# A split-weight decoder trunk on one core: weight low parts, bias steps and rotary products move to VectorE, and the planner gives VectorE and GpSimd one SBUF port

## The chip, the core and the metric

The kernel runs on one core of a Trainium2 chip. TensorE (PE) multiplies, VectorE (DVE), ScalarE (ACT) and GpSimd (POOL) do the elementwise work, and SyncE (SP) issues the loads. The metric is the device time of one execution in microseconds; lower is better.

## The reference

Two layers work on 256 tokens of width 1024. Each layer is a token mixer between two half-step SwiGLU blocks of inner width 2816.

```python
def swiglu(h, wg, wu, wd):
    return (jax.nn.silu(h @ wg) * (h @ wu)) @ wd

for i in range(DEPTH):                       # DEPTH = 2
    x = x + 0.5 * swiglu(rmsnorm(x, ffn_norm1[i]), ffn1_wg[i], ffn1_wu[i], ffn1_wd[i])
    h = rmsnorm(x, mix_norm[i])
    x = x + (sliding_window_attention(h, ...) if i % 2 == 0 else latent_attention(h, ...))
    x = x + 0.5 * swiglu(rmsnorm(x, ffn_norm2[i]), ffn2_wg[i], ffn2_wu[i], ffn2_wd[i])
```

Mixer A (layer 0) is causal attention over a window of 128 with 16 query heads and 2 key heads of 64, per-head norms of queries and keys, a sink per head, and a bias per head that depends on the distance of two positions through 32 buckets. Mixer B (layer 1) is latent attention: queries and keys/values come from low-rank projections (256 and 128 wide), each head has 64 plain and 32 rotary columns, and the rotary part is turned by the position:

```python
    q = rmsnorm(q, q_gain)
    q = jnp.concatenate([q[..., :QK_NOPE], apply_rope(q[..., QK_NOPE:], pos)], axis=-1)
```

## The kernel before

**Numbers.** Matrix products keep float32 accuracy by splitting. `weight` (L352) loads a weight tile of 128x1024 into `raw`; ScalarE rounds it into the high part `whi` (L371), and the remainder is the low part `wlo = raw - whi` (L366). Three matmuls (high by high, high by low, low by high) stand for one product. There are 301 such tiles: six per chunk of 256 inner columns in 44 chunks (264), and 37 in the mixers. `raw` has 5 buffers, `whi` and `wlo` 8 each.

**Stages.** In the trace they follow each other: first SwiGLU from 0 to about 250 us, mixer A from about 250 to 313, second SwiGLU to about 500, third SwiGLU to about 690, mixer B to about 785, last SwiGLU to the end. A SwiGLU starts with a norm for each tile of 128 tokens (L653 squares, L661 sum, L664 reciprocal root as a power on GpSimd, L672 scaled copy `p`, L640 transposes, L614/L686 high and low part `xs`), then runs chunk 0 for each tile apart (`th` L779, `h` L781) and chunks 1 to 10 for both tiles together (matmuls L807 and L753).

**Order.** `Plan` takes all operations with their engine, cost, operands and buffers, and schedules them ahead of time: at each step the ready operation with the earliest start plus penalty goes next on its engine. Every engine then runs its own list in that order, so an operation that waits holds up all that stands behind it on its engine. An operation with two engines goes to the one where it ends first. For low parts these are

```python
LOENG = ("DVE", "POOL")
op(LOENG, (c_dve(m), c_pool(m)), low, [(raw, key_), (hi, key_)], [(lo, key_)], seq="wlo", pen=pen, prio=pr, name="W")
```

and the plan sent 254 of the 301 to VectorE and 47 to GpSimd. The plan knows the engines as independent.

**Bias.** Mixer A's bias is made during the first SwiGLU. `keys` (L526) turns positions into thresholds `dk` and differences `df` on GpSimd. `split_bias` (L511) splits the difference table `relb` into three bf16 parts on GpSimd and copies them into the block diagonal of `bdiag` (L518). `bias_ops` then makes 0/1 steps: for query tile 0 with 32 compares of 128x128 (L559), for tile 1 with 32 pairs L562 and L564, all on VectorE. In each of 8 groups 24 small matmuls (L575) multiply steps by `bdiag`; L582 adds the mask.

**Rotary part.** `rope_tables` (L429) makes cosine and sine products with the gains on GpSimd. In `mixer_b` the query projection is copied out of PSUM with all 384 columns (L608 or L612) into `t`, and `rope` does four products and sums on GpSimd (L1179 twice, L1182, L1184) for each of 8 groups of four heads. The key's rotary part is scaled on GpSimd (L1146).

Of the kernel before, what the change touches and what calls it, by code (L numbers as in the profile page):

```python
# [277 lines left out]
def kernel(  # L278
# [110 lines left out]
    def rope_tables():  # L389
# [42 lines left out]
        for t in range(NT):  # L432
            for nm, g in (("q", gq), ("k", gk)):
                cc, ss = const([P, ROPE], f"cc{nm}{t}"), const([P, ROPE], f"ss{nm}{t}")

                def tables(t=t, g=g, cc=cc, ss=ss):
                    g1, g2 = g[:, HD : HD + HALF], g[:, HD + HALF : DQK]
                    sn, cs = scs[:, t, 0, :], scs[:, t, 1, :]
                    G.tensor_tensor(out=cc[:, :HALF], in0=g1, in1=cs, op=ALU.mult)
                    G.tensor_tensor(out=cc[:, HALF:], in0=g2, in1=cs, op=ALU.mult)  # L440
                    G.tensor_tensor(out=ss[:, HALF:], in0=g1, in1=sn, op=ALU.mult)
                    G.tensor_tensor(out=ss[:, :HALF], in0=g2, in1=sn, op=ALU.mult)
                    G.tensor_scalar(
# [53 lines left out]
    def bias_consts():  # L497
# [26 lines left out]
        qidx = buf("clo0", [P, P])  # L524
        dma(0.5, lambda: pi.t, positions[0].partition_broadcast(P), [pi], 1.0)

        def keys():
            G.tensor_copy(out=posq.t, in_=pi.t)
            pv = posq.rearrange("p (t k j) -> p t k j", t=NT, j=4)
            for j in range(4):  # L530
                sl = slice(j * NBKT, (j + 1) * NBKT)
# [4 lines left out]
                G.tensor_tensor(out=df[sl], in0=pv[sl, 0, :, j], in1=pv[sl, 1, :, j], op=ALU.subtract)  # L536
            G.iota(qidx.t, pattern=[[1, P]], base=0, channel_multiplier=0, allow_small_or_imprecise_dtypes=True)

        op("POOL", 3.5, keys, [pi, cols], [posq, dk, df, qidx], pen=1.0)
        K.update(bd=bd, posq=posq, dk=dk, df=df, qidx=qidx)  # L540
# [3 lines left out]
    def bias_ops(t, grp):  # L544


        q, dk, df, qidx, cols, bd = (K[n] for n in ("posq", "dk", "df", "qidx", "cols", "bd"))
# [1 line left out]
        n = 4 if t == 0 else 2
        for i0 in range(0, 8, n):  # L550
            ms = [buf("bm", [P, P]) for _ in range(n)] if t else []

            def fn(i0=i0, ms=ms):
                for i in range(i0, i0 + n):
# [795 lines left out]
```

## Time and profile before

| what | before |
|---|---|
| median of three runs | 980.85 us (979.95 to 980.9) |
| profiled execution | 979.95 us, of which the span of instructions is 978.2 us |
| TensorE busy | 935.4 us, 96% of the span |
| VectorE busy | 624.7 us, 64% |
| ScalarE busy | 474.8 us, 49% |
| GpSimd busy | 197.1 us, 20% |
| memory read | 157.92 MB, 163 GB/s over the span |

Busy time is what an engine spends in instructions; an engine that is busy throughout sets the end, and the idle time of the others costs nothing by itself. The granted clock is the share of TensorE's full speed that it was given in a stretch.

### The profile page before, as it was taken

The page shows a single profiled execution, that of the slowest core. Times are in us where ns is not written, and L with a number is a line of the kernel's source. Part 1 is how long each engine was busy: PE and PEld are TensorE (multiplying, and loading weights), DVE is VectorE, ACT ScalarE, POOL GpSimd, SP SyncE. Part 2 cuts the span into 40 slices and gives each one's busy share as a digit, 9 for nine tenths or more (in the row PEclk, how much of TensorE's full clock was granted, in tenths as well). Part 3 has the DMA queues.
Part 4 walks back from the last instruction along what each step waited for, and adds up shares of the span by engine and source line. Part 5 has one row for each costly group of instructions (what it writes and reads, how often), then busy time and mean ns, then how long its engine had stood idle before and what let it go on. Part 6 is the DMA issues. An engine that isn't in the chain of part 4 may idle for free.

```text
span 978.2 us, 16592 instructions
## 1 busy us (share of the span) xinstructions
PE 935.4 (96%) x6318; PEld 841.0 (86%) x6318; DVE 624.7 (64%) x1161; ACT 474.8 (49%) x814; POOL 197.1 (20%) x218
## 2 busy tenths in 40 slices
PE   5979999999799999999999999999998989999998
PEld 3869989998666899999979999999887869999997
DVE  6588985566866765656576565646689575455552
ACT  5534353545665444444355443545688445354440
POOL 4275430105302110000020000000596021011010
PEclk8999999999889999999999999999999989999999
DMA  7655556564402585656554666564413175656541
GB/s 258 202 160 155 173 174 214 161 197 139 151 1 69 171 259 160 208 170 209 179 173 149 197 196 192 173 212 147 156 53 92 60 234 166 213 163 204 165 150 44
DMA packets 119630, 160.04 MB, mean 164 GB/s; under 512 B 9264, under 2 KB 102912, under 8 KB 119552
## 3 DMA queue, kind: packets, MB, share of 16 engines
q1 hardware_dynamic: 119552, 159.00, 51.7%
q8 instruction: 49, 0.80, 0.3%
q14 instruction: 29, 0.24, 0.1%
HBM read 157.92 MB, written 1.05 MB: 163 GB/s over the span
## 4 chain that ended last, share of the span: by engine, by line
PE 84%; DVE 6%; POOL 4%; issue 3%; ACT 2%; DMA 0%; SPq 0%; POOLq 0%; DVEq 0%; ACTq 0%
PE w L807 44%; PE acc L753 23%; PE w L640 2%; PE acc L707 2%; PE acc L708 2%; PE acc L709 2%; PE w L709 2%; PE w L707 2%; PE w L708 2%; DVE p L672 1%; PE w L1014 1%; DVE p L559 1%; POOL wlo L366 1%; POOL st L599 1%; DVE wlo L366 1%
## 5 line engine op out<-in xcount | busy, mean ns | idle before, releaser
L807 PE MATMUL w<-xs,whi 128*128 128x256 f32 x2560 | 456.3, 281 | 0.0
L807 PEld LDWEIGHTS w<-xs,whi 128*128 128x128 f32 x2560 | 393.1, 188 | 2.8
L366 DVE TENSOR_TENSOR wlo<-raw,whi 128x1024 fp32r<-128x1024 f32 (+3 forms) x254 | 309.9, 1236 | 99.8 <-ACT whi L371 99.2
L371 ACT CAST whi<-raw 128x1024 fp32r<-128x1024 f32 (+3 forms) x301 | 310.1, 1039 | 124.2 <-PE acc L753 91.4
L807 PE MATMUL w<-xs,wlo 128*128 128x256 f32 x1280 | 357.0, 279 | 0.0
L807 PEld LDWEIGHTS w<-xs,wlo 128*128 128x128 f32 x1280 | 241.5, 189 | 0.0
L366 POOL TENSOR_TENSOR wlo<-raw,whi 128x1024 fp32r<-128x1024 f32 (+1 forms) x47 | 120.6, 2575 | 253.6 <-ACT whi L371 231.3
L813 ACT ACTIVATE th<-w 128x256 f32<-128x256 f32 x80 | 30.7, 383 | 201.5 <-PE w L807 201.4
L815 DVE SCALAR_TENSOR_TENSOR th<-th,w 128x256 f32<-128x256 f32 x80 | 33.4, 418 | 133.1 <-ACT th L813 133.1
L753 PE MATMUL acc<-whi,pT 128*128 128x512 f32 x352 | 113.2, 395 | 0.0
L753 PE MATMUL acc<-wlo,pT 128*128 128x512 f32 x352 | 112.7, 394 | 0.0
L753 PE MATMUL acc<-whi,t 128*128 128x512 f32 x352 | 112.3, 392 | 0.0
L753 PEld LDWEIGHTS acc<-wlo,pT 128*128 128x128 f32 x352 | 66.4, 189 | 15.2
L753 PEld LDWEIGHTS acc<-whi,t 128*128 128x128 f32 x352 | 66.0, 188 | 15.6 <-DVE t L626 0.4
L753 PEld LDWEIGHTS acc<-whi,pT 128*128 128x128 f32 x352 | 63.3, 188 | 11.5
L608 ACT CAST pT<-h 128x256 fp32r<-128x256 f32 x80 | 32.5, 406 | 64.5 <-DVE h L817 64.1
L821 DVE TENSOR_TENSOR t<-h,pT 128x256 fp32r<-128x256 f32 x80 | 39.3, 491 | 36.4 <-ACT pT L608 36.4
L664 POOL TENSOR_TENSOR rstd<-var,mhalf 128x1 f32<-128x1 f32 x8 | 4.4, 550 | 233.3 <-DVE var L661 233.3
L699 POOL TENSOR_TENSOR var<-ss 128x1 f32<-128x1 f32 x4 | 0.8, 195 | 205.1 <-ACT junk L653 205.1
L640 PE MATMUL w<-ident,p 128*128 128x128 f32 x160 | 27.4, 309 | 14.4 <-DVE p L672 12.3
L640 PEld LDWEIGHTS w<-ident,p 128*128 128x128 f32 x160 | 20.4, 156 | 22.8 <-DVE p L672 14.8
L707 PE MATMUL w<-whi,xs 128*128 128x512 f32 (+2 forms) x96 | 39.3, 409 | 0.6 <-DVE xs L614 0.6
(186 smaller groups left out, 952.6 us busy)
## 6 DMA issues: line engine op xcount, KB each, us to landing
raw<-in_ffn_wd_dram SPq DMA_DIRECT2D x88, 512.0 KB, 4.4
raw<-in_ffn_wg_dram SPq DMA_DIRECT2D x175, 256.0 KB, 3.9
raw<-in_ffn_wu_dram SPq DMA_DIRECT2D x175, 256.0 KB, 4.2
raw<-in_a_w_in_dram SPq DMA_DIRECT2D x10, 512.0 KB, 4.5
raw<-in_a_w_out_dram SPq DMA_DIRECT2D x8, 512.0 KB, 3.6
raw<-in_b_w_out_dram SPq DMA_DIRECT2D x8, 512.0 KB, 3.6
raw<-in_b_w_in_dram SPq DMA_DIRECT2D x4, 416.0 KB, 3.6
raw<-in_b_w_uq_dram SPq DMA_DIRECT2D x4, 384.0 KB, 3.6
```

The source lines that it names most:

```text
L366: (V if e == "DVE" else G).tensor_tensor(out=lo[:, c], in0=raw[:, c], in1=hi.t.bitcast(F32)[:, c], op=ALU.subtract)
L371: op("ACT", c_act(m), lambda c=c: A.copy(out=hi[:, c], in_=raw[:, c]), [(raw, key_)], [(hi, key_)], seq="wh", pen=pen, prio=pr, name="W")
L608: A.copy(out=o(), in_=i())
L640: T.transpose(out=dst[:rows, i * P : (i + 1) * P], in_=src(i), identity=ident.t)
L707: T.matmul(o, lhsT=hi, rhs=wh, start=start, stop=False)
L708: T.matmul(o, lhsT=hi, rhs=wl, start=False, stop=False)
L709: T.matmul(o, lhsT=lo, rhs=wh, start=False, stop=stop)
L753: T.matmul(acc[nh].t, lhsT=a[:, ft, t0 : t0 + P], rhs=wt[:, nh * 512 : (nh + 1) * 512], start=(c == 0 and ft == 0 and i == 0), stop=(final ...
L807: T.matmul(o, lhsT=wt[:, sl], rhs=xs[:, p, :, kt], start=(kt == j == i == 0), stop=(kt == KT - 1 and j == 1 and i == 2))
L813: op("ACT", c_act(FC, 0.05), lambda th=th, ps=ps: A.activation(th.t, ps[:, :FC], AF.Tanh, scale=0.5), [ps], [th], name=nm)
L815: op("DVE", 0.345, lambda th=th, ps=ps: V.scalar_tensor_tensor(out=th.t, in0=th.t, scalar=1.0, in1=ps[:, :FC], op0=ALU.add, op1=ALU.mult), ...
L821: op("DVE", 0.36, lambda h=h, hthi=hthi, htlo=htlo, fb=fb: V.tensor_tensor(out=htlo[:, fb], in0=h.t, in1=hthi[:, fb].bitcast(F32), op=ALU. ...
```

## The change

The low part has one engine now, VectorE. The plan gets one more resource: an operation of GpSimd, or one of VectorE that reads nothing from PSUM, doesn't start before the last such operation of the other engine has ended. The rotary tables, `keys`, `split_bias`, the query's rotary part and the key's rotary scaling go from GpSimd to VectorE. The query's rotary products read PSUM, so the copy takes 256 columns in place of 384. The steps of tile 0 are one compare of 128x1024 for each of 4 groups. Those of tile 1 are, for each of 8 half groups, four `Sign` and four `Identity` activations of 128x128 on ScalarE (64 in all) and one compare of 128x512 on VectorE. Lines of the changed kernel stand 7 to 16 further down: L366 is L373 there, L559 is L567, L575 is L591, L614 is L630, L672 is L688.

```diff
-LOENG = ("DVE", "POOL")
+BSPEN = 2.0
...
+        o.port = not any((b[0] if isinstance(b, tuple) else b).tag in ("w", "acc0", "acc1") for b in r)
...
+            if e == "POOL" or (e == "DVE" and o.port):
+                s = max(s, self.port["DVE" if e == "POOL" else "POOL"])
             done = s + cost + (POOLPEN if e == "POOL" and len(alts) > 1 else 0.0)
...
-                op(LOENG, (c_dve(m), c_pool(m)), low, [(raw, key_), (hi, key_)], [(lo, key_)], seq="wlo", pen=pen,
+                op("DVE", c_dve(m), low, [(raw, key_), (hi, key_)], [(lo, key_)], seq="wlo", pen=pen,
...
         def split_bias():
+            V.tensor_scalar(out=blk.t, in0=qidx[:, :4], scalar1=cols[:, 1:2], scalar2=None, op0=ALU.is_equal)
             for i, b16 in enumerate(parts):
-                G.tensor_copy(out=b16.t, in_=r.t)
+                V.tensor_copy(out=b16.t, in_=r.t)
                 if i < 2:
-                    G.tensor_tensor(out=r.t, in0=r.t, in1=b16.t, op=ALU.subtract)
-                for j in range(4):
-                    sl = slice(j * NBKT, (j + 1) * NBKT)
-                    G.tensor_copy(out=bd[sl, i, :, j], in_=b16[sl, :])
-
-        op("POOL", 3.5, split_bias, [], [r, bd] + parts, pen=1.0, name="bd")
+                    V.tensor_tensor(out=r.t, in0=r.t, in1=b16.t, op=ALU.subtract)
+                V.tensor_tensor(out=bd[:, i], in0=b16.t.unsqueeze(2).broadcast_to([P, H, 4]),
+                                in1=blk.t.unsqueeze(1).broadcast_to([P, H, 4]), op=ALU.mult)
+
+        op("DVE", 1.0, split_bias, [cols, qidx], [r, bd, blk] + parts, pen=1.0, name="bd")
...
+        if t == 0:
+            op("DVE", c_dve(1024), lambda: V.tensor_tensor(
+                out=steps.t, in0=qt(8), in1=heads(dk[:, 0, grp * 8 : grp * 8 + 8], 8, P), op=ALU.is_ge),
+               [q, dk], [steps], pen=BSPEN, name="bs")
+        for i0 in (0, 4) if t else ():
+            m = buf("p", [P, 4, P])
+
+            def fn(i0=i0, m=m):
+                for i in range(4):
+                    k = grp * 8 + i0 + i
+                    A.activation(m[:, i], qidx.t, AF.Sign, bias=nj[:, k : k + 1])
+                for i in range(4):
+                    k = grp * 8 + i0 + i
+                    A.activation(m[:, i], m[:, i], AF.Identity, bias=df[:, k : k + 1], scale=hd[:, k : k + 1])
+
+            op("ACT", 8 * c_act(P, 0.02), fn, [nj, qidx, df, hd], [m, (steps, i0)], pen=BSPEN, name="bs")
+            op("DVE", c_dve(512), lambda i0=i0, m=m: V.tensor_tensor(
+                out=steps[:, i0 : i0 + 4], in0=qt(4), in1=m.t, op=ALU.is_ge),
+               [q, m], [(steps, i0)], pen=BSPEN, name="bs")
...
-            op("POOL", 0.36, lambda: G.tensor_tensor(
+            op("DVE", 0.2, lambda: V.tensor_tensor(
                 out=kn[:, :, HD:], in0=heads(rr[:, :4], 4, ROPE),
...
-            op(AV, (0.37, 0.47), copy_scaled(lambda: qn.t, qv), [qb], [qn], name=name)
+            op(AV, (0.26, 0.34), copy_scaled(lambda: qn[:, :, :HD], lambda: qv()[:, :, :HD]), [qb], [(qn, 0)], name=name)
...
-                    G.tensor_tensor(
-                        out=tmp[:, :, a0 : a0 + HALF], in0=qn[:, :, HD + b0 : HD + b0 + HALF],
+                    V.tensor_tensor(
+                        out=tmp[:, :, a0 : a0 + HALF], in0=qv()[:, :, HD + b0 : HD + b0 + HALF],
```

What the plan makes of it on VectorE just ahead of the first bias matmuls, before: the compares L559 stand in front of the copy of the table (`relb`, L508) and the rest of `split_bias` is on GpSimd.

```order
L559 TENSOR_SCALAR p<-chi_562,dk 128x128 x24
L815 SCALAR_TENSOR_TENSOR th<-th,w 128x256
L817 TENSOR_TENSOR h<-w,th 128x256
L559 TENSOR_SCALAR p<-chi_562,dk 128x128 x4
L821 TENSOR_TENSOR t_700<-h,pT 128x256
L559 TENSOR_SCALAR p<-chi_562,dk 128x128 x4
L508 COPY relb<-w 128x16
L366 TENSOR_TENSOR wlo<-raw,whi 128x1024 x2
```

In the change the same table is copied and split on VectorE before the first `th` of chunk 1:

```order
L517 COPY relb<-w 128x16
L373 TENSOR_TENSOR wlo<-raw,whi 128x1024
L524 TENSOR_SCALAR blk<-clo_106,cols 128x4
L526 CAST relb_473<-relb 128x16
L528 TENSOR_TENSOR relb<-relb,relb_473 128x16
L529 TENSOR_TENSOR bdiag<-relb_473,blk 128x64
...
L526 CAST relb_475<-relb 128x16
L529 TENSOR_TENSOR bdiag<-relb_475,blk 128x64
L373 TENSOR_TENSOR wlo<-raw,whi 128x1024 x2
L831 SCALAR_TENSOR_TENSOR th<-th,w 128x256
```

So `bdiag` is complete two chunks earlier in VectorE's list, and no longer behind the compares. The first bias group itself stands 48 L807 matmuls later in TensorE's list than before.

On GpSimd around the two norms of the first SwiGLU, before: a low part stands right behind the reciprocal root of tile 0, and four more behind that of tile 1.

```order
L664 TENSOR_TENSOR rstd_137<-var_132,mhalf 128x1
L366 TENSOR_TENSOR wlo<-raw,whi 128x1024
L664 TENSOR_TENSOR rstd_217<-var_213,mhalf 128x1
L366 TENSOR_TENSOR wlo<-raw,whi 128x1024 x4
L528 CAST chi_562<-chi_504 128x256
```

In the change the two roots follow each other, and nothing of 128x1024 is left in GpSimd's list; the other three SwiGLU blocks read alike.

```order
L680 TENSOR_TENSOR rstd_140<-var_135,mhalf 128x1
L680 TENSOR_TENSOR rstd_220<-var_216,mhalf 128x1
L485 TENSOR_SCALAR nsink<-sink 128x16
L487 TENSOR_SCALAR ka<-gcol 128x1
L499 MEMSET kb 128x1
```

On VectorE where mixer B ends and the last SwiGLU begins (L626 makes `xs` low parts, L924 and, in the change, L940 add the mixer's output into `x`), before:

```order
L892 TENSOR_SCALAR p<-p,st 128x256 x2
L626 TENSOR_TENSOR xs<-acc_8254,xs 128x512
L612 CAST xs<-acc_8445 128x512
L626 TENSOR_TENSOR xs<-acc_8445,xs 128x512
L366 TENSOR_TENSOR wlo<-raw,whi 128x1024
L626 TENSOR_TENSOR xs<-acc_8508,xs 128x512
L924 TENSOR_TENSOR x_64<-acc_8386,x_64 128x512
```

The low part shown is one of the eight of `b_w_out`; of the others VectorE's list held two 15 and 7 rows ahead of it and two more than a hundred rows ahead, and GpSimd's list three. In the change all eight stand here in VectorE's list:

```order
L373 TENSOR_TENSOR wlo<-raw,whi 128x1024
L900 RECIPROCAL st<-st 128x4
L908 TENSOR_SCALAR p<-p,st 128x256 x2
L373 TENSOR_TENSOR wlo<-raw,whi 128x1024 x4
L642 TENSOR_TENSOR xs<-acc_8396,xs 128x512
L373 TENSOR_TENSOR wlo<-raw,whi 128x1024 x3
L940 TENSOR_TENSOR x_64<-acc_8431,x_64 128x512
```

They moved from two engines and a spread of places to one engine and one place, beside the 72 matmuls that use them.

## Rows read from the trace of the kernel before

**Rows 1.** The page's chain that ended last, shares of the span by engine

```profile
PE 84%; DVE 6%; POOL 4%; issue 3%; ACT 2%; DMA 0%; SPq 0%; POOLq 0%; DVEq 0%; ACTq 0%
```

**Rows 2.** Windows by stage: length, busy us (instructions) of each engine, granted clock, DMA share, GB/s

```profile
0.00:30.00 30.00, 18.43 (x58) 13.45 (x59) 18.03 (x38) 16.22 (x29) 13.44 (x20) 0.89 0.70 228
30.00:75.00 45.00, 38.41 (x280) 35.29 (x279) 32.34 (x71) 18.26 (x26) 22.46 (x35) 0.94 0.63 194
75.00:222.00 147.00, 147.00 (x1158) 136.32 (x1158) 109.08 (x202) 65.09 (x91) 40.81 (x39) 1.00 0.56 178
...
255.00:285.00 30.00, 24.42 (x105) 16.53 (x104) 24.45 (x112) 16.70 (x66) 5.23 (x3) 0.77 0.16 51
...
313.00:330.00 17.00, 13.98 (x59) 10.72 (x58) 15.97 (x24) 7.98 (x12) 7.79 (x4) 0.90 0.60 185
...
705.00:735.00 30.00, 27.12 (x186) 23.66 (x186) 26.09 (x85) 25.50 (x71) 28.01 (x52) 1.00 0.24 72
735.00:760.00 25.00, 22.41 (x202) 18.89 (x202) 23.74 (x77) 21.31 (x60) 15.26 (x17) 1.00 0.35 106
...
785.00:808.00 23.00, 18.67 (x90) 15.40 (x89) 17.21 (x24) 9.58 (x17) 5.12 (x2) 0.85 0.70 218
```

**Rows 3.** Waits of TensorE: line, what it waited for, us in total, times, longest

```profile
PE w L640 <- DVE p L672: 12.3, 7, 3.5
PE w L575 <- POOL bdiag L518: 6.6, 3, 3.3
PE w L1014 <- DVE st L857: 4.7, 1, 4.7
...
PE w L640 <- DVE h L781: 3.9, 2, 3.4
```

**Rows 4.** Timeline of VectorE: start, us, operation [idle before <-releaser]

```profile
15.75 5.04 DVE L672 TENSOR_SCALAR p<-x,rstd 128x512 f32<-128x512 f32 x2 [0.67 <-POOL rstd L664]
...
256.70 1.25 DVE L857 SCALAR_TENSOR_TENSOR st<-st,nsink 128x4 f32<-128x4 f32 x1
257.98 2.27 DVE L860 TENSOR_TENSOR st<-sink,st 128x4 f32<-128x4 f32 x1
260.17 0.15 DVE L857 SCALAR_TENSOR_TENSOR st<-st,nsink 128x4 f32<-128x4 f32 x1
...
771.54 0.88 DVE L672 TENSOR_SCALAR p<-x,rstd 128x512 f32<-128x512 f32 x2 [0.66 <-POOL rstd L664]
```

**Rows 5.** Timeline of GpSimd at the same two places

```profile
15.69 4.83 POOL L366 TENSOR_TENSOR wlo<-raw,whi 128x1024 fp32r<-128x1024 f32 x2
...
255.57 4.65 POOL L366 TENSOR_TENSOR wlo<-raw,whi 128x1024 fp32r<-128x1024 f32 x2
```

**Rows 6.** Groups of VectorE by form: busy us, mean ns | idle before

```profile
L366 DVE TENSOR_TENSOR wlo<-raw,whi 128x1024 fp32r<-128x1024 f32 x245 | 301.5, 1248 | 98.5 <-ACT whi L371 97.9 <-PE w L807 0.2
...
L562 DVE TENSOR_SCALAR bm<-clo,cols,df 128x128 f32<-128x128 f32 x32 | 16.0, 500 | 0.0
L564 DVE SCALAR_TENSOR_TENSOR p<-bm,dk,chi 128x128 bf16<-128x128 f32 x32 | 15.5, 485 | 1.1
...
L559 DVE TENSOR_SCALAR p<-chi,dk 128x128 bf16<-128x128 f32 x32 | 11.0, 418 | 1.7 <-POOL dk L532 1.7
...
L582 DVE TENSOR_TENSOR S<-w,upper 128x128 f32<-128x128 f32 x16 | 3.5, 279 | 0.0
...
L1143 DVE TENSOR_TENSOR knb<-acc,st 128x256 f32<-128x256 f32 x8 | 3.4, 421 | 1.1 <-POOL st L599 0.9
...
L612 DVE COPY S<-w 96x512 f32<-96x512 f32 x3 | 2.0, 681 | 0.5 <-PE w L640 0.5
```

**Rows 7.** Groups of GpSimd by form, the same columns

```profile
L366 POOL TENSOR_TENSOR wlo<-raw,whi 128x1024 fp32r<-128x1024 f32 x46 | 118.8, 2591 | 253.6 <-ACT whi L371 231.3 <-PE w L807 16.6 <-PE w L709 5.2
L599 POOL TENSOR_TENSOR st<-st,mhalf 128x4 f32<-128x4 f32 x16 | 16.8, 1062 | 2.4 <-DVE st L884 0.9 <-DVE st L1140 0.8 <-DVE st L1172 0.7
```

**Rows 8.** One group of ScalarE by form, the same columns

```profile
L610 ACT ACTIVATE xs<-w,gcols 128x128 fp32r<-128x128 f32 x52 | 14.9, 366 | 21.6 <-PE w L640 16.9 <-DVE xs L614 4.7
```

More of the change, by code (lines that the diff above doesn't have):

```diff
@@ L91 @@
     __slots__ = ("eng", "cost", "fn", "deps", "bufs", "prio", "seq", "end", "tail", "pen", "name", "users", "nd",
-                 "eng_used")
+                 "eng_used", "port")
     def __init__(self, **k):
@@ L220, in run @@
         self.ticks = {}
+        self.port = {"DVE": 0.0, "POOL": 0.0}
         while left:
@@ L261, in run @@
             o.end = free[e] = s + cost
+            if e == "POOL" or (e == "DVE" and o.port):
+                self.port[e] = o.end
             for b in o.bufs:
@@ L438, in tables @@
                     sn, cs = scs[:, t, 0, :], scs[:, t, 1, :]
[L439 to L443, printed above, removed]
+                    V.tensor_tensor(out=cc[:, :HALF], in0=g1, in1=cs, op=ALU.mult)
+                    V.tensor_tensor(out=cc[:, HALF:], in0=g2, in1=cs, op=ALU.mult)
+                    V.tensor_tensor(out=ss[:, HALF:], in0=g1, in1=sn, op=ALU.mult)
+                    V.tensor_tensor(out=ss[:, :HALF], in0=g2, in1=sn, op=ALU.mult)
+                    V.tensor_scalar(
                         out=ss[:, :HALF], in0=ss[:, :HALF], scalar1=-1.0, scalar2=None, op0=ALU.mult
                     )
-                op("POOL", 0.8, tables, [g, scs], [cc, ss], pen=1.0)
+                op("DVE", 0.45, tables, [g, scs], [cc, ss], pen=1.0)
                 K[f"cc{nm}", t], K[f"ss{nm}", t] = cc, ss
@@ L531, in keys @@
                 sl = slice(j * NBKT, (j + 1) * NBKT)
-                G.tensor_scalar(
+                V.tensor_scalar(
                     out=dk[sl], in0=pv[sl, :, :, j], scalar1=cols[sl, 0:1], scalar2=None, op0=ALU.add
                 )
[L536 to L540, printed above, removed]
+                V.tensor_tensor(out=df[sl], in0=pv[sl, 1, :, j], in1=pv[sl, 0, :, j], op=ALU.subtract)
+            V.tensor_scalar(out=nj.t, in0=cols[:, 1 : 1 + P // 4], scalar1=-1.0, scalar2=0.5, op0=ALU.mult, op1=ALU.add)
+            V.tensor_scalar(out=hd.t, in0=df.t, scalar1=0.5, scalar2=None, op0=ALU.mult)
+            V.tensor_tensor(out=df.t, in0=dk[:, 1], in1=hd.t, op=ALU.subtract)
+        op("DVE", 1.6, keys, [pi, cols], [posq, dk, df, nj, hd], pen=1.0)
+        K.update(bd=bd, posq=posq, dk=dk, df=df, qidx=qidx, nj=nj, hd=hd)
         K["bias0"] = buf("S8", [P, H, P])
@@ L544, in bias_ops @@
     def bias_ops(t, grp):
-        q, dk, df, qidx, cols, bd = (K[n] for n in ("posq", "dk", "df", "qidx", "cols", "bd"))
+        q, dk, df, qidx, nj, hd, bd = (K[n] for n in ("posq", "dk", "df", "qidx", "nj", "hd", "bd"))
         steps = buf("p", [P, 8, P], BF16)
[L549 to L554, printed above, removed]
-                    kk = grp * 8 + i
-                    d = dk[:, t, kk : kk + 1]
-                    qt = q[:, t * P : (t + 1) * P]
-                    if t == 0:
-                        V.tensor_scalar(out=steps[:, i], in0=qt, scalar1=d, scalar2=None, op0=ALU.is_ge)
-                    else:
-                        m = ms[i - i0].t
-                        V.tensor_scalar(out=m, in0=qidx.t, scalar1=cols[:, 1 + kk : 2 + kk],
-                                        scalar2=df[:, kk : kk + 1], op0=ALU.is_lt, op1=ALU.mult)
-                        V.scalar_tensor_tensor(
-                            out=steps[:, i], in0=m, scalar=d, in1=qt, op0=ALU.add, op1=ALU.is_le
-                        )
-            op("DVE", n * (0.15 if t == 0 else 0.645), fn, [q, dk, df, qidx, cols], [(steps, i0)] + ms, pen=0.5, name="bs")
@@ L1178, in rope @@
                     a0, b0 = i * HALF, (1 - i) * HALF
-                    G.tensor_tensor(
-                        out=tmp[:, :, a0 : a0 + HALF], in0=qn[:, :, HD + b0 : HD + b0 + HALF],
+                    V.tensor_tensor(
+                        out=tmp[:, :, a0 : a0 + HALF], in0=qv()[:, :, HD + b0 : HD + b0 + HALF],
                         in1=sn[:, a0 : a0 + HALF].unsqueeze(1).broadcast_to([P, 4, HALF]), op=ALU.mult)
-                G.tensor_tensor(out=qn[:, :, HD:], in0=qn[:, :, HD:],
+                V.tensor_tensor(out=qn[:, :, HD:], in0=qv()[:, :, HD:],
                                 in1=cc.t.unsqueeze(1).broadcast_to([P, 4, ROPE]), op=ALU.mult)
-                G.tensor_tensor(out=qn[:, :, HD:], in0=qn[:, :, HD:], in1=tmp.t, op=ALU.add)
-            op("POOL", 1.62, rope, [K["ssq", t], K["ccq", t]], [qn, tmp], name=name)
+            op("DVE", 0.6, rope, [qb, K["ssq", t], K["ccq", t]], [(qn, 1), tmp], name=name)
+            op("DVE", 0.2, lambda: V.tensor_tensor(out=qn[:, :, HD:], in0=qn[:, :, HD:], in1=tmp.t, op=ALU.add),
+               [tmp], [(qn, 1)], name=name)
             qns.append(qn)
```

16 lines of the change are left out of this document (9 added, 7 removed).

## The prediction

> **What bounds the kernel now.** I read first the chain of work that ended last, then the windows by stage, then what TensorE waited for, and last the timelines at those waits. The chain is TensorE's for 84% and VectorE's and GpSimd's for 10% together [rows 1]: the reader is to see that the end is set by matmuls, and by the few places where they stand still. The windows say where [rows 2]. From 75 to 222 us TensorE is busy for 147.00 of 147.00 us at a granted clock of 1.00, so whatever gets cheaper there gives nothing. Time can come back only where TensorE is idle or its clock is below 1.00: at 0 to 30 (18.43 of 30 busy, clock 0.89), 30 to 75 (38.41 of 45, 0.94), 255 to 285 (24.42 of 30, 0.77), 313 to 330 (13.98 of 17, 0.90), 705 to 760 (49.53 of 55, 1.00) and 785 to 808 (18.67 of 23, 0.85). The waits name the releasers [rows 3]: 12.3 us for the norm's scaled copy `p`, 6.6 us for GpSimd's `bdiag`, 4.7 us for the small sink operations ahead of L1014, 3.9 us for `h`.
>
> **Why `p` and the sink operations are late.** The timeline shows a pair of `p` in 0.88 us at 771.54, and in 5.04 us at 15.75 [rows 4]. The second pair runs while GpSimd makes two low parts, from 15.69 for 4.83 us [rows 5]; the two engines end together. At 256.70 and 257.98 two operations on 128x4 numbers take 1.25 and 2.27 us, and 0.15 for the same line a little later [rows 4]; GpSimd makes two low parts there too, from 255.57 for 4.65 us [rows 5]. So a low part on GpSimd makes some VectorE operations wait for its end. The Trainium skill (SBUF — State Buffer, section on the two separate sides) has this as a lock on a shared port pair, held for a whole instruction by whichever of VectorE and GpSimd starts first; the 5.04 us against 0.88 agree.
>
> **The change, term by term.** The sum is made against the profiled execution, 979.95 us, which is 0.9 us below the median 980.85.
>
> *Norms of the four SwiGLU blocks.* No low part stands behind the reciprocal root on GpSimd any more. A `p` beside a low part was (5.04 - 0.88) / 2 = 2.1 us longer than alone [rows 4]. The longest wait for `p`, 3.5 us [rows 3], falls to about 1.4. The other six, 8.8 us together, are short of or about one such stretch each, and I leave 1.9 us of them for the links that stay (squares, sum, root). That is 12.3 - 1.4 - 1.9 = 9.0 us. Bounds: -5, if these links keep more than half, and -12.3, all of it. I take -9.
>
> *`bdiag`.* The 6.6 us are GpSimd's conversions and copies, which could start only when the table had come out of VectorE's list behind the compares. Now all of it stands on VectorE two chunks earlier and the bias matmuls come 48 matmuls later; the first compare of 128x1024 costs about one low part, 1.25 us [rows 6]. I take the whole -6.6; bounds -4 (a late compare or constant) and -6.6.
>
> *Mixer A.* The stretches of 1.1 and 2.1 us [rows 4] lie in the wait of 4.7 [rows 3]: -3.2, bounds 0 (the next link is as late) and -4.7.
>
> *`h`.* The waits of 3.9 us [rows 3] stand at the starts of SwiGLU blocks, behind low parts in VectorE's list. Those get shorter where GpSimd held them, but five to seven now stand in a row: -2, bounds 0 and -3.9.
>
> *Clock.* Every window below 1.00 holds one of these waits, and 705 to 760, with 5.5 us of idle time in small pieces, stays at 1.00 [rows 2]. Below the upper level of 2.4 GHz the five windows lack 0.11 x 30 + 0.06 x 45 + 0.23 x 30 + 0.10 x 17 + 0.15 x 23 = 18 us [rows 2]. Part of this lies in the idle time itself and part in mixer A, where idle time stays. I take -4; bounds 0 and -9.
>
> *Low parts on VectorE alone.* 47 at 1.25 us [rows 6] in place of 2.59 us on GpSimd [rows 7] are 59 us more for VectorE. In 75 to 222 it was busy for 109.08 of 147 [rows 2], and there the old steps fall away. So no steady chunk waits. At the start one low part of the first weights now stands ahead of the second tile's `p`: +1 (bounds 0 and +2.5, two low parts). At the block starts low parts come one behind another at 1.25 us: +1.5 (bounds 0 and +5, four of them uncovered).
>
> *Bias steps.* L559, L562 and L564 were 11.0 + 16.0 + 15.5 = 42.5 us of VectorE [rows 6]. In their place stand 4 compares at 1.25 and 8 of half that width at about 0.68 (the 96x512 row [rows 6]), 10.4 us, and 64 activations at 0.366 [rows 8], 23 us of ScalarE. ScalarE had 82 us idle in 75 to 222 [rows 2], and that is the cover. If one half group of eight came uncovered it would cost 2.9 us; I take 0, bounds 0 and +3.
>
> *Mixer B.* This is the term I know least. VectorE was busy for 49.83 of 55 us from 705 to 760, ScalarE for 46.81, GpSimd for 43.27 [rows 2]. VectorE gets, for 8 groups, four rotary operations and one key product, 128x64 to 128x128, each 0.28 (128x128) [rows 6] or a little less: 40 x 0.27 = 11 us; by the row of 128x256 at 0.42 [rows 6] at most 17. It loses nine copies and scalings that the plan now puts on ScalarE, 0.42 to 0.68 each [rows 6], about 5.5 us, a few low parts that now come later, and stretches by GpSimd. VectorE's list is thus about as long as before, ScalarE's is 5 us longer, and both are near full. All eight low parts of `b_w_out` then follow in one place: 10 us of VectorE, the first one or two ahead of any matmul that needs them. Bounds: -5.5 (all idle time of the stretch goes) and +8 (11 us of rotary work, less some 3 us of stretches). I take +2, nearer to the middle than to either, since the list's length hardly changes and only the tail is new.
>
> Sum: -9 - 6.6 - 3.2 - 2 - 4 + 1 + 1.5 + 0 + 2 = -20.3; 979.95 - 20.3 = 959.65, and 960 beside the runs.
>
> **Rivals.** (a) *Mixer B is bound by VectorE*: 90% busy before [rows 2], and it gets the most there. At its upper bound the sum is 6 us worse, 966; with 3 us of late low parts, 969. For it: both helpers near full. Against: the plan gave copies to ScalarE. Chance 0.17.
> (b) *The norms don't come back*: the change lifts the stretch, but five to seven low parts in VectorE's list stand where GpSimd worked beside it, and hold `th`, `h` and `xs` as long. Then the terms of norms, `h` and clock fall away, -6.6 - 3.2 + 1 + 1.5 + 2 = -5.3, 975; with half of the norms 970. Against: the list has `p` ahead of them. Chance 0.12.
> (c) *The clock follows fully*: -9 in place of -4, and mixer B's idle time shrinks by 3 in place of +2: 950. Chance 0.08.
> (d) *GpSimd's roots get later*: what a low part of GpSimd did to VectorE, one of VectorE does to GpSimd. A root that meets a low part starts up to 1.25 us late, eight roots of the norms 10 us: 970. Against: the 16 roots of 128x4 take 1.06 us on average [rows 7] though VectorE is 90% busy around them. Chance 0.05. The lock of the Trainium skill (SBUF — State Buffer, same section) works in both directions and would have it so; no run here shows it yet.
> (e) *Slower*: in mixer B nothing is hidden. Place: 705 to 785. 11 us of rotary work, 5 low parts more (6.2), the 5.5 us of copies that ScalarE can't take at once either, and three low parts of `b_w_out` that GpSimd used to make (3.7) come to 26 us in place of +2: 984. It decides from 22 us of added waits on. For it: three engines near full at once. Against: TensorE's own idle time there is 5.5 us, so part of any delay was covered before. Chance 0.06.
> My forecast as summed has 0.52, with a range of its own of 953 to 967.
>
> **How the numbers follow.** A difference of 0.2% (2 us) is about what a measurement of this kernel can tell from none. Faster by more: all but (e) and the tails of (a) and (b), 0.91. Slower by more: 0.06. Within: 0.03. The range 950 to 973 reaches to (c) below and to (a), (d) and the better half of (b) above; outside are (e), the worse half of (b), and half of (c), with the tails 0.18.
>
> **What would show it.** In the profile after, every pair of `p` takes about 0.9 us, and TensorE's wait for it falls from 12.3 to about 3. The wait for `bdiag` is gone, and bias matmuls run at clock 1.00. L857 and L860 (L873 and L876 there) stay at 0.15, with a wait ahead of the scores of about 1.5. The steady windows stay at 100% busy. VectorE's total comes to 624.7 + 59 - 42.5 + 10.4 + 11 - 5.5 = 657 us less the stretches, so 630 to 655. I am wrong if the stage from 705 to 785 gets longer by more than 8 us, if TensorE waits for low parts for more than 5 us in all, or if `p` still takes 2 us without GpSimd beside it.

## The result and the profile after

The changed kernel took 967.72 us (median of four, 965.01 to 970.03) against 980.74 us before: ratio 0.9868, interval 0.9836 to 0.9899, 13 us faster. The profiled execution is the slowest of the four, 970.03 us with a span of 968.2, while that of the kernel before was its fastest; the two profiles lie 10 us apart, and the stages below add up to that.

The page of the changed kernel: its busy times, and its chain.

```profile
PE 937.1 (97%) x6318; PEld 839.3 (87%) x6318; DVE 623.7 (64%) x1192; ACT 502.8 (52%) x891; POOL 46.2 (5%) x84
...
PE 84%; DVE 7%; DMA 3%; ACT 2%; issue 2%; SPq 1%; POOL 1%; POOLq 0%; DVEq 0%; ACTq 0%
```

GpSimd's 197.1 us became 46.2, VectorE's total stayed (623.7 after 624.7). TensorE's longest waits:

```profile
PE w L1282 <- DMA grow<-in_ffn_norm_dram: 4.7, 1, 4.7
PE w L724 <- DVE wlo L373: 3.3, 2, 1.8
PE w L656 <- DVE p L688: 3.2, 2, 1.6
PE w L591 <- DVE p L567: 2.4, 1, 2.4
PE w L1228 <- DVE S L628: 1.9, 2, 1.2
PE acc L1242 <- DVE pT L628: 1.8, 3, 1.0
PE w L656 <- DVE h L797: 1.7, 2, 0.9
PE w L1030 <- ACT st L892: 1.5, 1, 1.5
```

Beside [rows 3] the reader sees `p` at 3.2 in place of 12.3, `h` at 1.7 in place of 3.9, the wait ahead of the scores (L1014, now L1030) at 1.5 in place of 4.7 and ended by a ScalarE operation, and `bdiag` gone. The wait for the load of `grow` stood at 4.2 us before. New are 3.3 us for low parts (0.3 on this line and tile before), 2.4 us for the first compare (L567), and several short waits in mixer B. The windows by stage (the columns of [rows 2]):

```profile
0.00:30.00 30.00, 21.49 (x84) 16.46 (x84) 18.82 (x44) 16.66 (x32) 3.48 (x16) 1.00 0.76 247
30.00:75.00 45.00, 42.55 (x317) 40.17 (x318) 35.81 (x93) 26.76 (x46) 5.48 (x4) 0.96 0.71 209
75.00:222.00 147.00, 147.00 (x1133) 135.21 (x1132) 102.14 (x170) 83.51 (x145) 2.85 (x10) 1.00 0.55 172
222.00:255.00 33.00, 31.04 (x177) 25.95 (x176) 24.17 (x78) 19.25 (x44) 7.98 (x6) 0.95 0.47 160
255.00:285.00 30.00, 30.00 (x125) 20.04 (x125) 18.54 (x73) 19.18 (x69) 0.00 (x0) 0.83 0.11 36
...
705.00:735.00 30.00, 26.99 (x209) 22.39 (x208) 24.92 (x106) 26.60 (x73) 9.03 (x9) 1.00 0.18 54
735.00:760.00 25.00, 22.03 (x149) 17.21 (x149) 19.46 (x45) 15.42 (x39) 1.01 (x1) 1.00 0.52 165
760.00:785.00 25.00, 21.59 (x99) 16.68 (x98) 17.37 (x39) 10.11 (x21) 1.10 (x2) 1.00 0.21 63
```

The start is busier and its first 30 us are at full clock, the steady stretch is as full as before, and mixer B (from about 680 us now) has more idle time. VectorE's groups of the operations in question:

```profile
L688 DVE TENSOR_SCALAR p<-x,rstd 128x512 f32<-128x512 f32 x16 | 7.1, 483 | 5.5 <-POOL rstd L680 5.5
L567 DVE TENSOR_TENSOR p<-chi,dk 128x1024 bf16<-128x1024 f32 x4 | 4.9, 1220 | 0.0
...
L1192 DVE TENSOR_TENSOR qrt<-w,ssq 128x64 f32<-128x64 f32 x16 | 2.8, 217 | 1.5 <-ACT sqq L1184 1.4
...
L876 DVE TENSOR_TENSOR st<-sink,st 128x4 f32<-128x4 f32 x8 | 1.3, 165 | 0.3
L873 DVE SCALAR_TENSOR_TENSOR st<-st,nsink 128x4 f32<-128x4 f32 x8 | 1.2, 151 | 0.1
```

All sixteen `p` take 0.48 us, and no operation of 128x4 is stretched. VectorE's timeline shows why the first compare is late:

```profile
60.38 0.17 DVE L409 CAST posf<-posi 128x2 f32<-128x2 int32 x1 [2.83 <-DMA posi<-in_positions_dram]
...
69.54 1.22 DVE L567 TENSOR_TENSOR p<-chi,dk 128x1024 bf16<-128x1024 f32 x1
```

VectorE stands for 2.83 us for the load of the positions that the rotary tables need, an operation ahead of the compare in its list. TensorE then starts the bias matmuls at 70.81, 2.45 us late.

To place the gain I cut each trace at five ends of down-projection matmuls (L753, L769 in the changed kernel), which every kernel below has. The columns are the first SwiGLU; mixer A with the first chunk behind it; the second and third SwiGLU; mixer B with the first chunk behind it; the rest of the last SwiGLU. Each row is one profiled execution, in us; the last two columns are the median of the timed runs and the ratio to the kernel before, timed beside it on the same chip, with its 95% interval. The runs lie on several chips, so kernels are compared by their ratios.

| kernel | first | A | 2nd, 3rd | B | rest | median | ratio |
|---|---|---|---|---|---|---|---|
| before | 223.0 | 122.7 | 349.0 | 114.1 | 165.7 | 980.74 | |
| changed | 215.1 | 116.3 | 348.0 | 119.0 | 166.2 | 967.72 | 0.9868 (0.9836 to 0.9899) |
| e1 low parts made by VectorE | 216.2 | 118.0 | 348.7 | 112.4 | 165.7 | 964.54 | 0.9817 (0.9792 to 0.9841) |
| e2 bias alone | 216.3 | 122.9 | 349.0 | 114.2 | 165.7 | 974.79 | 0.9920 (0.9898 to 0.9943) |
| e3 changed, rotary on GpSimd | 213.2 | 116.7 | 348.0 | 122.3 | 166.2 | 971.84 | 0.9885 (0.9862 to 0.9908) |
| e4 changed, six raw buffers | 211.7 | 114.7 | 348.0 | 118.6 | 166.1 | 964.17 | 0.9804 (0.9779 to 0.9829) |
| e5 changed, no port in the plan | 211.5 | 114.5 | 348.0 | 114.8 | 166.1 | 960.65 | 0.9779 (0.9754 to 0.9805) |
| e6 bias and low parts | 211.0 | 114.5 | 348.7 | 110.2 | 165.7 | 956.69 | 0.9744 (0.9720 to 0.9769) |
| e7 e6 with rotary on VectorE | 210.4 | 114.5 | 348.7 | 117.1 | 165.7 | 962.85 | 0.9812 (0.9785 to 0.9839) |
| e8 e6, six raw buffers | 210.6 | 118.3 | 348.7 | 113.6 | 165.7 | 958.37 | 0.9764 (0.9738 to 0.9790) |
| e9 changed, positions early | 210.0 | 114.8 | 347.0 | 118.2 | 165.7 | 963.22 | 0.9803 (0.9768 to 0.9837) |
| e10 e5 with rotary on GpSimd | 211.1 | 114.7 | 348.0 | 109.7 | 167.6 | 956.71 | 0.9720 (0.9685 to 0.9756) |
| e11 e6, positions early | 210.6 | 117.0 | 348.7 | 111.4 | 165.7 | 960.07 | 0.9762 (0.9728 to 0.9797) |
| e12 e10, positions early | 209.4 | 110.5 | 347.0 | 110.3 | 167.1 | 953.02 | 0.9727 (0.9705 to 0.9750) |

The changed kernel wins 7.9 us in the first SwiGLU and 6.4 in mixer A, and loses 4.9 in mixer B. By the same cuts TensorE's idle time went from 18.2 to 11.0 us, from 8.6 to 2.4 and, in mixer B, from 9.9 to 13.1, while its busy time moved by less than 2 us in each column. (The first SwiGLU's last matmul ends at 223 us; the stretch from there to 250 us, counted to it ahead of the prediction, belongs to mixer A.) The first column is one execution and carries its scatter: changed, e3, e5 and e10 have the same TensorE order there and stand at 215.1, 213.2, 211.5 and 211.1.

### The profile page after: what moved, and what is told of

Its sections match the earlier page's. It is cut to its first block, busy times and chain, and to the rows that moved or that the text cites. A ratio compares the mean times of both kernels' runs of the same rounds, so it can differ in the third digit from the quotient of the medians.

```text
span 968.2 us, 16489 instructions
## 1 busy us (share of the span) xinstructions
PE 937.1 (97%) x6318; PEld 839.3 (87%) x6318; DVE 623.7 (64%) x1192; ACT 502.8 (52%) x891; POOL 46.2 (5%) x84
## 4 chain that ended last, share of the span: by engine, by line
PE 84%; DVE 7%; DMA 3%; ACT 2%; issue 2%; SPq 1%; POOL 1%; POOLq 0%; DVEq 0%; ACTq 0%
PE w L823 44%; PE acc L769 24%; PE w L656 3%; DVE wlo L373 2%; PE acc L723 2%; PE acc L725 2%; PE acc L724 2%; PE w L724 2%; PE w L725 2%; PE w L723 2%; PE w L1030 1%; ACT p L887 1%; PE acc L1056 1%; PE w L591 1%; SPq L370 1%
## 5 line engine op out<-in xcount | busy, mean ns | idle before, releaser
L373 DVE TENSOR_TENSOR wlo<-raw,whi 128x1024 fp32r<-128x1024 f32 (+3 forms) x301 | 357.4, 1212 | 86.9 <-ACT whi L378 86.5
L769 PE MATMUL acc<-whi,t 128*128 128x512 f32 x352 | 113.8, 397 | 0.0
L769 PE MATMUL acc<-wlo,pT 128*128 128x512 f32 x352 | 113.2, 396 | 0.0
L769 PE MATMUL acc<-whi,pT 128*128 128x512 f32 x352 | 112.9, 394 | 0.0
L769 PEld LDWEIGHTS acc<-whi,t 128*128 128x128 f32 x352 | 66.1, 188 | 15.8
L769 PEld LDWEIGHTS acc<-wlo,pT 128*128 128x128 f32 x352 | 66.2, 188 | 14.9
L769 PEld LDWEIGHTS acc<-whi,pT 128*128 128x128 f32 x352 | 63.1, 188 | 12.3
L837 DVE TENSOR_TENSOR t<-h,pT 128x256 fp32r<-128x256 f32 x80 | 34.0, 426 | 37.0 <-ACT pT L624 37.0
L724 PE MATMUL w<-wlo,xs 128*128 128x512 f32 (+2 forms) x96 | 36.8, 383 | 3.3 <-DVE wlo L373 3.3
L723 PE MATMUL acc<-whi,xs 128*128 128x512 f32 x96 | 39.3, 410 | 0.0
L724 PE MATMUL acc<-wlo,xs 128*128 128x512 f32 x96 | 38.2, 398 | 0.5 <-DVE wlo L373 0.4
L725 PE MATMUL acc<-whi,xs 128*128 128x512 f32 x96 | 38.1, 397 | 0.4 <-DVE xs L642 0.4
L723 PE MATMUL w<-whi,xs 128*128 128x512 f32 (+2 forms) x96 | 37.4, 390 | 0.2 <-DVE xs L630 0.2
L725 PE MATMUL w<-whi,xs 128*128 128x512 f32 (+2 forms) x96 | 37.0, 385 | 0.3 <-DVE xs L702 0.3
```

The lines of the kernel that those rows point to most:

```text
L373: V.tensor_tensor(out=lo[:, c], in0=raw[:, c], in1=hi.t.bitcast(F32)[:, c], op=ALU.subtract)
L723: T.matmul(o, lhsT=hi, rhs=wh, start=start, stop=False)
L724: T.matmul(o, lhsT=hi, rhs=wl, start=False, stop=False)
L725: T.matmul(o, lhsT=lo, rhs=wh, start=False, stop=stop)
L769: T.matmul(acc[nh].t, lhsT=a[:, ft, t0 : t0 + P], rhs=wt[:, nh * 512 : (nh + 1) * 512], start=(c == 0 and ft == 0 and i == 0), stop=(final ...
L837: op("DVE", 0.36, lambda h=h, hthi=hthi, htlo=htlo, fb=fb: V.tensor_tensor(out=htlo[:, fb], in0=h.t, in1=hthi[:, fb].bitcast(F32), op=ALU. ...
```

## The experiments

My theory was that low parts on GpSimd had stretched VectorE's operations, that the bias had held TensorE up by its own wait, and that VectorE's rotary work made mixer B longer. The rivals: another cause of the long `p`; weights that come late in mixer B since raw buffers are held until their low part is made; the order that the plan makes with the port.

**e1, low parts made by VectorE.** The kernel before, every order kept; the 47 low parts planned for GpSimd are issued on VectorE at their place.

```diff
-                    (V if e == "DVE" else G).tensor_tensor(
+                    V.tensor_tensor(
```

> The kernel before with its plan and every engine's order unchanged, except that the 47 low parts planned for GpSimd are made by VectorE at the same place of the program. If low parts on GpSimd hold VectorE up (my reading): every pair of the norm's p takes about 0.9 us, TensorE's wait for p falls from 12.3 to about 4 us, the two sink operations take 0.15 us each, the wait of 6.6 us for bdiag stays; 966 to 973 us. If the long p had another cause (the late root, memory traffic): p stays at 2 us or more, and the time is within 2 us of before or above it, since VectorE has 59 us more to do.

964.54 us, ratio 0.9817: 18 us by the ratio, where the whole change gives 13, though the two intervals touch. (The two profiled executions lie 13.4 us apart.) Its busy times, its groups on VectorE and TensorE's waits:

```profile
PE 932.9 (97%) x6318; PEld 838.3 (87%) x6318; DVE 632.9 (66%) x1208; ACT 475.0 (49%) x814; POOL 79.5 (8%) x171
```

```profile
L672 DVE TENSOR_SCALAR p<-x,rstd 128x512 f32<-128x512 f32 x16 | 7.1, 484 | 5.5 <-POOL rstd L664 5.5
...
L860 DVE TENSOR_TENSOR st<-sink,st 128x4 f32<-128x4 f32 x8 | 1.3, 162 | 0.3
```

```profile
PE w L575 <- POOL bdiag L518: 4.4, 2, 3.3
...
PE w L640 <- DVE p L672: 3.5, 3, 1.8
```

Nothing but the engine of 47 instructions differs, and `p` falls from 1.27 to 0.48 us on average, its wait from 12.3 to 3.5. The cause of the long `p` is shown. The wait for `bdiag`, which I expected to stay at 6.6, fell to 4.4; what shortened it isn't separated. VectorE was given 47 low parts more, 57 us at 1.22 us each, and its busy time rose by only 8.2 (632.9 after 624.7). So by an estimate from these totals VectorE had stood for almost 50 us beside GpSimd's low parts, about 1 us for each: nearly what it costs VectorE to make one itself. The time lies below the range that I gave this run.

**e2, the bias alone.** The kernel before with the changed `bias_consts` and `bias_ops` (the part of the diff that begins at `split_bias`).

> The kernel before with the changed bias alone (table split and thresholds on VectorE, wide compares, signs on ScalarE), planned anew; low parts and rotary part as before. My reading: the wait for bdiag (6.6 us) goes, a wait of about 2.4 us for the first compare comes, as in the changed kernel; the waits for p stay near 12 us; 973 to 977 us. If the bias is worth its whole wait and its clock: 971 to 973. If ScalarE's 64 activations are not covered: 980 or more.

974.79 us, ratio 0.9920, 8 us; all of it in the first SwiGLU (216.3 after 223.0), every later stage as long as before. The wait for the first compare is 1.3 us, less than the 2.4 expected. Its `p` stays long:

```profile
L683 DVE TENSOR_SCALAR p<-x,rstd 128x512 f32<-128x512 f32 x16 | 19.7, 1270 | 5.4 <-POOL rstd L675 5.4
```

**e3, rotary part on GpSimd.** The changed kernel with the four GpSimd operations of `rope`, the key's product and the full copy of the query as before; the order is the changed kernel's up to mixer B.

```diff
-            op("DVE", 0.6, rope, [qb, K["ssq", t], K["ccq", t]], [(qn, 1), tmp], name=name)
+            op("POOL", 1.62, rope, [K["ssq", t], K["ccq", t]], [qn, tmp], name=name)
```

> The changed kernel with the query's rotary part and the key's rotary scaling back on GpSimd (and the full copy of the query); the order is the changed kernel's until mixer B. If VectorE's 11 us of rotary work are what made mixer B longer (my reading): the stretch from the end of the third SwiGLU to the output projection falls from 69.7 to about 66 us and the time by 3 to 5 us against the changed kernel. If the low parts and weights that come late are it: the stretch stays within 1 us, and the time within 2 us of the changed kernel's 967.7; if GpSimd's rotary products hold VectorE up instead, it gets longer.

The stretch with mixer B got longer, 122.3 after 119.0, and the time did not fall (0.9885 against 0.9868, intervals overlap). Its window over that stretch (columns as above):

```profile
677.90:800.20 122.30, 109.81 (x652) 90.12 (x652) 85.76 (x225) 81.26 (x198) 37.87 (x80) 0.96 0.30 95
```

The granted clock is 0.96 here and 1.00 in the changed kernel; TensorE's idle time, 12.5 us, is about the changed kernel's 13.1. So the 3.3 us more may be the clock of one execution. My theory of mixer B fell as stated: with the changed plan, taking the rotary work off VectorE doesn't help.

**e4, six raw buffers.** `NRAW` 6 in place of 5 in the changed kernel.

> The changed kernel with six buffers for raw weights in place of five, planned anew. If the loads of the output projection and of the last SwiGLU come late because a raw buffer is held until VectorE has made its low part: DMA moves more between 680 and 740 us, and mixer B with the start of the last SwiGLU gets 3 to 5 us shorter, 963 to 965. If VectorE's rotary work is the cause: within 2 us of 967.7.

964.17 us, ratio 0.9804: a time in the range that I gave for late weights, but by luck, for mixer B stayed at 118.6. What was won lies in the first SwiGLU and mixer A, where another order was planned and where e5 gets the same lengths with five buffers. The rival of late weights falls as the cause in mixer B.

**e5, no port in the plan.** The changed kernel, every operation on the same engine, without the two lines that make one engine wait for the other in the plan.

```diff
-            if e == "POOL" or (e == "DVE" and o.port):
-                s = max(s, self.port["DVE" if e == "POOL" else "POOL"])
```

> The changed kernel without the port in the plan (GpSimd and VectorE planned as independent again); all engines of operations as in the changed kernel, the order the same until mixer A. If the port in the plan is what made mixer B longer, by an order that spares collisions which the hardware hardly charges: the stretch from the end of the third SwiGLU to the first chunk of the last one falls from 119.0 to about 114 us, the time by 4 to 6 us against the changed kernel. If planning all low parts for VectorE is what made it longer: it stays at 118 to 120, the time within 2 us.

960.65 us, ratio 0.9779: by the ratios 9 us below the changed kernel, with intervals apart. In the profiles mixer B is 4.2 us shorter; mixer A, where the orders part, 1.8. The rest lies in the first SwiGLU, which has the same TensorE order, and so can't be put down to the port. One profile of mixer B carries some us of its own: e8 stands at 113.6 and e6 at 110.2, with the same work in it and a granted clock of 0.97 against 1.00. But the four profiles planned with the port stand at 118.2 us or more (changed, e3, e4, e9), and the ten planned without it at 109.7 to 117.1, of which e7 is the longest.

**e6, e7, e8: the winning parts together.** e6 is e2 with e1's line. e7 is e5 with low parts planned for both engines and issued on VectorE, so it differs from e6 by the rotary part. e8 is e6 with `NRAW` 6.

> The two parts that won alone, together: the changed bias, and low parts planned for both engines as before but all made by VectorE; rotary part on GpSimd and no port in the plan. If the two gains (17.5 and 7 us) lie in different waits, they add: 955 to 960 us, with mixer B as long as in the kernel with low parts alone (112 us from the third SwiGLU's end to the first chunk of the last). If they share a wait or the clock behind it: 960 to 964.

> The changed kernel, rotary part on VectorE included, but planned without the port and with low parts for both engines; all low parts are made by VectorE. Against the run without the rotary part it tells what that part is worth. If VectorE's rotary work costs time when the low parts come early: 3 to 5 us above that run. If it is neutral or better than GpSimd's: within 2 us or below, 953 to 960 us.

> Bias and low parts as in the run with those two alone, with six raw buffers. If the sixth buffer helps since loads otherwise wait for VectorE's low parts: 2 to 4 us below that run. If it helped the changed kernel by another order of its first SwiGLU only: within 2 us of it.

e6: 956.69 us, ratio 0.9744. Alone the two parts gave 1.83% and 0.80%, together 2.56%: they add. e7 takes 962.85, with mixer B at 117.1 in place of 110.2: without the port in the plan VectorE's rotary work, with the order planned for it, does cost about 6 us. The sixth buffer helped nothing (958.37).

**e9, positions early.** The changed kernel, with the load of the rotary positions asked for first among the small constants.

```diff
-        dma(0.5, lambda: pos_i.t, positions[0].rearrange("(t p) -> p t", p=P), [pos_i], 1.0)
+        dma(0.5, lambda: pos_i.t, positions[0].rearrange("(t p) -> p t", p=P), [pos_i], 1.0, 0)
```

> The changed kernel with one load, the positions for the rotary tables, asked for some 20 microseconds earlier; the order of TensorE differs in 16 rows. If VectorE's 2.83 us of standing before the rotary angles are what makes the first compare, and with it the first bias matmul, late: that idle time goes, TensorE's wait for the compare falls from 2.4 us to under 1 us, the clock behind it stays up, 963 to 966 us with less spread between runs. If the compare is late for the low parts ahead of it: the wait stays, 966 to 969.

963.22 us, ratio 0.9803; its interval overlaps the changed kernel's at the edge. VectorE's timeline in e9:

```profile
50.61 0.16 DVE L409 CAST posf<-posi 128x2 f32<-128x2 int32 x1
...
67.12 1.22 DVE L567 TENSOR_TENSOR p<-chi,dk 128x1024 bf16<-128x1024 f32 x1
```

The cast waits for nothing, the compare comes 2.4 us earlier, and TensorE's wait for it is gone from the list. The scatter stayed (961.14 to 967.72), so that part of the expectation failed.

**e10, the fourth cell.** e3 and e5 together: rotary part on GpSimd, no port in the plan, low parts planned for VectorE.

> The changed kernel without the port in the plan and with the rotary part back on GpSimd; low parts planned for VectorE alone. Fills the fourth cell beside the changed kernel (119.0 us from the third SwiGLU's end to the first chunk of the last), rotary part on GpSimd with the port (122.3) and on VectorE without it (114.8). If the port in the plan and the rotary work on VectorE each cost on their own: 110 to 112 us there, 955 to 958 in all. If early planned low parts, not the rotary part, made the short stretch of 110.2: 114 to 117, 959 to 963.

956.71 us, ratio 0.9720; mixer B takes 109.7. The four cells of that stretch are 119.0 and 122.3 with the port (rotary part on VectorE, on GpSimd) and 114.8 and 109.7 without. The windows over the stretch, first of the changed kernel, then of e5, then of e10 (columns as above):

```profile
679.30:798.30 119.00, 105.92 (x653) 87.02 (x652) 90.78 (x269) 79.32 (x195) 23.08 (x40) 1.00 0.32 98
```

```profile
674.00:788.80 114.80, 105.26 (x653) 87.56 (x652) 92.19 (x277) 76.41 (x187) 25.46 (x40) 0.99 0.32 102
```

```profile
673.80:783.60 109.80, 102.37 (x641) 85.39 (x640) 87.52 (x241) 72.44 (x181) 41.61 (x80) 1.00 0.33 102
```

TensorE idles for 13.1, 9.5 and 7.4 us, VectorE for 28.2, 22.6 and 22.3, and ScalarE is busy for 79.3, 76.4 and 72.4 us: with the port the plan leaves VectorE standing more. It also gives ScalarE more of the copies and scalings that either engine can do: 64 of 108 in the changed kernel and 67 in e3, against 56 in e5 and 51 in e10. Did the hardware ask for that? GpSimd in e10, then VectorE at the same places:

```profile
679.68 2.02 POOL L1120 TENSOR_TENSOR krt<-kr,ssk 128x16 f32<-128x16 f32 x2 [0.95 <-DVE kr L1112]
...
701.68 3.43 POOL L613 TENSOR_TENSOR st<-st,mhalf 128x4 f32<-128x4 f32 x3
...
712.68 0.46 POOL L1193 TENSOR_TENSOR t<-t,ccq 128x128 f32<-128x128 f32 x1
```

```profile
679.51 2.11 DVE L371 TENSOR_TENSOR wlo<-raw,whi 128x768 fp32r<-128x768 f32 x2
...
702.41 0.86 DVE L906 TENSOR_SCALAR p<-p,st 128x128 f32<-128x128 f32 x4
...
711.36 0.60 DVE L906 TENSOR_SCALAR p<-p,st 128x256 f32<-128x256 f32 x2
...
712.41 0.88 DVE L906 TENSOR_SCALAR p<-p,st 128x256 f32<-128x256 f32 x2
```

Four scalings run in 0.86 us beside two of three roots of GpSimd. Shape by shape, the scalings of that stage beside a root alone are no longer than those with GpSimd idle: 128x128 takes 0.27 to 0.29 us in both cases, 128x256 0.34 and 0.35 (the pair at 711.36 is beside a root). A rotary product does hold VectorE: of the pair at 712.41 the second scaling takes 0.61 us beside it. It is the one VectorE operation beside GpSimd in this trace that is more than 0.1 us longer than others of its line and shape. Otherwise GpSimd is the one that waits: two products of 128x16 take 2.02 us beside two low parts. In e5, planned without the port, the 16 roots take 1.0 to 1.06 us each. The plan's rule, which makes either engine wait for all of the other, charges for collisions that mostly don't happen. That this is why its order is longer is my reading; no run kept the rule for the colliding operations alone.

**e11 and e12: earlier positions in the best two.**

> The best kernel so far (changed bias; low parts planned for both engines and made by VectorE; rotary part on GpSimd; no port in the plan) with the load of the rotary positions earlier. If that load also delays VectorE here: 954 to 956 us against 956.7. If it is hidden here: within 1 us.

> The changed kernel without the port in the plan, with the rotary part on GpSimd, and with the rotary positions loaded earlier: what the single runs showed to help, together. If they are separate waits: 1 to 3 us below the 956.7 of the run without the earlier load, 953 to 956. If the first compare was hardly late in that run: within 1 us of it.

e11 took 960.07 us, 3 us above e6 where I expected no more than 1; by the ratios, 0.9762 against 0.9744, the intervals overlap. Its mixer A takes 117.0: nothing won. e12 has the lowest median, 953.02, but its ratio 0.9727 (0.9705 to 0.9750) is that of e10 and, within the intervals, of e6. These three beat both kernels; which of them is best isn't settled.

## Why the prediction was right, and which terms were off

The direction and the range held: 967.72 lies in 950 to 973, 13 us of the 20 forecast came. The forecast as summed had a range of its own, 953 to 967, and that was missed by 0.7 us; the time lies where rival (a) put it, 966 to 969. The wide range held in part by luck: it covered a clock term that the profiles do not show and a cost in mixer B for which the sum had no term. By its steps:

*Norms* (-9): right. The wait fell from 12.3 to 3.2 us, the mean `p` from 1.27 to 0.48, and e1 shows that the low parts on GpSimd were the cause. Rival (b) is out.

*Mixer A* (-3.2): right in the wait, 4.7 to 1.5, and the two operations take 0.15 to 0.17 us. The stage won 6.4 us with the norm behind it.

*`h`* (-2): 3.9 to 1.7, right.

*Bias steps on ScalarE* (0): right. The stretch from 75 to 222 us is full, 147.00 of 147.00, with 64 more activations in it. They took 0.390 and 0.481 us on average, more than the 0.366 I read for them.

*`bdiag`* (-6.6): the mechanism was right, the size off. 2.4 us of the 6.6 came back as a wait for the first compare, -4.2 net. I had named a late constant as the bound and then taken the whole; the constant was the positions' load, behind which VectorE stood, as e9 shows. Alone (e2) the part is worth 8 us.

*Clock* (-4): the granted clock rose, but the balance of the two profiles doesn't show its 4 us. The windows after lack 0.04 x 45 + 0.05 x 33 + 0.17 x 30 = 8.6 us, 9.4 less than the 18 before, near rival (c). Yet TensorE's busy time did not fall, 937.1 us after 935.4; its idle time fell from 42.8 to 31.1 us, which is more than the 10.0 us between the two spans. How much of the clock's gain lies inside the idle time that went isn't separated.

*Low parts on VectorE* (+2.5 in two terms): the waits for them came to 3.7 us (3.3 and 0.4 in two rows), after 1.1 before (0.8 and 0.3): right. e1 shows the part as a whole to be worth 18 us by the ratio and 13.4 between the profiles; the terms of norms, mixer A, `h` and clock with these +2.5 come to -15.7. VectorE's total, 623.7 us, came out below the 630 to 655 that I named, because the stretches that went had taken more than the 2 to 27 us that this range allows for: almost 50 us by e1.

*Mixer B* (+2): this is the step that failed, in size and in what it was made of. The stretch got 4.9 us longer, although shares of the norm, `h` and clock terms fell into it. I costed VectorE's rotary work (11 us forecast; 9.4 by the groups: 2.8 for L1192 and three times 2.2), and I counted the copies and scalings that go to ScalarE (nine forecast, ten in the trace) as relief. I had no term at all for the new resource of the plan, which reorders mixer B. e5 takes it out: 4.2 us in this stage, 9 us in all by the ratios, of which the scatter of the first SwiGLU holds some. Rival (a) has the right place, and e6 against e7 shows its price without the port, about 6 us; with the port no run shows the rotary part on VectorE to be worse than on GpSimd (e3). Rival (e), a slower kernel, would have needed 26 us there.

*Rival (d)*: GpSimd's operations do get longer beside VectorE's low parts, two products at 2.02 us in e10, but the waits that follow from it stay short. The Trainium skill (SBUF — State Buffer, section on the two separate sides) has the lock work both ways for a whole instruction: the low parts on either engine agree, and GpSimd's roots, beside which VectorE's scalings kept their 0.86 us for four, do not.

What stays open: the changed kernel scatters over 5 us between executions (965.01 to 970.03) where the kernel before stayed within 1 us beside it, though it too scattered more on other chips (979.37 to 985.64 beside e1). The profiles put part of it into the first SwiGLU (211.1 to 215.1 us for one TensorE order). The first weights land at different times there: ScalarE gets to the same early weight tile, behind its load, at 9.5 us in the changed kernel, at 10.7 in e3 and at 9.1 in e5. And the wait for the first compare differs: 2.4 us in the changed kernel, with a granted clock of 0.91 from 70 to 90 us behind it, but 0.9, 1.2 and 0.4 us in e3, e5 and e10, with 1.00. e9 removed this wait and not the scatter. The mixers scatter too: against e6, e8 has 3.8 us more in mixer A and 3.4 in mixer B, e11 2.5 and 1.2. TensorE's idle time there is the same within 0.5 us; the granted clock is lower, in mixer A 0.94 and 0.96 against 0.99. What sets it, the plan or the execution, no run here separates.

## What to carry to other kernels

When a cheap operation is long now and then, look what the engine that shares its memory port does at that moment: here 47 low parts on a slow engine that looked 80% idle cost 18 us, and moving them to the engine that seemed busier added 8 us to its busy time and not 57, because it had been standing beside them. Put a conflict into a planner's model only for the operations whose rows show it: the plans with a rule that made all pairs exclusive were 4 to 13 us longer in the stage where VectorE and ScalarE have the most to do (part of the 13 is the clock of one execution). And an edit to a scheduler's model is an edit to the kernel: it needs a term in the sum.

## What was not expected of the hardware

The hold-up depends on the kind of operation. A low part on GpSimd (2.6 us) held VectorE's scaled copies of 128x512 (0.48 to 2.6 us) and sums of 128x4 (0.15 to 2.3 us), and a rotary product on GpSimd (0.46 us) one scaling of 128x256 (0.35 to 0.61 us). A root on GpSimd (1.0 us for 128x4) held nothing on VectorE that the trace of e10 shows, not even low parts (1.22 us beside it), and became longer itself beside VectorE's work there, up to 1.48 us. The profile's spans of GpSimd are rough.
